# A layer kernel's opening written out anew by pairs of blocks, and a second pool for half of the raw h

## The chip, the cores and the metric

The kernel runs on one core of one Trainium2 chip. The metric is the device time of one execution in microseconds (us); lower is better. The profile is of one execution; the median is of three timed runs.

## The reference, cut to what matters

The layer is a mixer on 1024 tokens of width 2048:

```python
mod = jax.nn.silu(c) @ w_ada[layer] + b_ada[layer]
shift, scale, gate = jnp.split(mod, 3, axis=-1)
h = rms_norm(x, norm_gain[layer]) * (1.0 + scale[:, None, :]) + shift[:, None, :]
proj = h @ w_in[layer]            # (1024 x 2048) @ (2048 x 8192)
...                               # two groups of heads on proj
y = jnp.concatenate([oa, ob], axis=-1).astype(x.dtype) @ w_out[layer]
x = x + (gate[:, None, :] * y).astype(x.dtype)
```

So before the first product with `w_in` there must be the whole `x` (8 MB), its norms, and of `w_ada` (2048 x 6144) the columns of shift and scale for those parts of the width that are used first.

## The kernel before

**The products.** Each big product is made by a Strassen-like scheme with seven products per group of 256 output columns, `P1` to `P7`. Left factors are sums of quarters of h (`A11`, `S3`, `S2`, `A12`, `S1`, `A22`, `S4`; `LEFT` says which product takes which), right factors sums of quarters of the weights (`RIGHT`). Each left factor consists of four tiles of 128x512, one for each pair j = 0 to 3 of 128-blocks of the width (`NP` = 4). Left and right are split in a high and a low part (fp32r), and `mm3` makes three matmuls: high x high, high x low, low x high. One product is 4 pairs x 3 = 12 matmuls, a group 84. `plan` writes the order of products (`flat`) and hangs onto each (product, pair) the making of weights (`Group.make`, `first`, `second`). `run` issues 12 matmuls for a product, does the events, and after each pair calls `tick`, by which loads, stores and side tasks go out in a written order. Groups e (`groups_a`, 16 of them, the first half of the width) come first, then f and g (`groups_b`, second half), h, y and o.

**The opening** (lines 448 to 588). The SP queue loads 32 tiles of x, then `ada_a` tiles: 16 rows for each pair j (each row is 128 x 512 numbers, 256 KB). PE turns x by matmuls against `dg`, diagonal matrices that hold the norms (`turn_x`: 4 matmuls of 128x128 for each of 16 blocks and two halves g of the tokens). For each pair, the 16 rows are weighted with silu(c) and summed: rows 0, 3, 6, 8, 11, 14 by VectorE (`weigh`), rows 5 and 13 by ScalarE and GpSimd, the other 8 by PE (`ada_rows_pe`); `ada_finish` sums over partitions and makes `a_c` and `s_c` (`ada_mod`). `first_half(j)` makes h of the pair (`to_h`, ScalarE), its sums (`combine`, on GpSimd; on VectorE for the last pair), and splits all seven into high and low (`place`: high on ScalarE, L146, low on VectorE, L147). Only after `first_half(3)` does the first group begin: P1, P6, P7, P2, P5. In this stretch only PE's order is as written; the order of the other engines is the scheduler's. From line 599 on every engine's order is as written.

**The seam after groups_a** (lines 657 to 699). While the 16 groups run, side tasks make the second half of h. At the end `gather` places the new left factors as the old ones fall free (`place_later`, at most one in two ticks). Last come `A22` and `S4`: they take the place of factors that are used by the last two products of the last e group, and the raw tiles that they are made of (`a11`, which becomes S2 and then S4, and `a22`) stay in the pool `k1`. The next pool, `hs`, for the heads, takes the same memory; so before it is opened, `until(groups_b[0], "P7")` and `drain()` issue all that is left to place:

```python
    until(groups_b[0], "P7")
    drain()
    k1p2.__exit__(None, None, None)
    k1p.__exit__(None, None, None)
```

Of the kernel before, what the change touches and what calls it, by code (L numbers as in the profile page):

```python
# [17 lines left out]
P = 128  # L18
# [22 lines left out]
ADA_DVE = (0, 3, 6, 8, 11, 14)  # L41
ADA_ACT = (5, 13)
# [17 lines left out]
def layer_kernel(ctx, tc, x, c, w_ada, b_ada, norm_gain, w_in, sb_q_gain, sb_k_gain, ret_norm_gain, w_out,  # L60
# [4 lines left out]
    ctx.enter_context(tc.manual_schedule(engines={mybir.EngineType.PE}))  # L65
# [34 lines left out]
    k1 = k1p.__enter__()  # L100
    stp = tc.tile_pool(name="st", bufs=1)
# [18 lines left out]
    nc.scalar.dma_start(rows[66:74, 0:P], ret_norm_gain.rearrange("o (k p) -> (o k) p", p=P))  # L120
    rows_ps = ps.tile([P, P], F32, tag="C", name="rows_ps")
# [82 lines left out]
    def combine(a11, a12, a21, a22, new, sub):  # L204

        s1, s2, s4 = (new(n) for n in ("S1", "S2", "S4"))
        sub.tensor_tensor(s1, a21, a22, op=ALU.add)
        sub.tensor_tensor(s2, s1, a11, op=ALU.subtract)
        sub.tensor_tensor(a21, a11, a21, op=ALU.subtract)
        sub.tensor_tensor(s4, a12, s2, op=ALU.subtract)  # L210
        return {"A11": a11, "S3": a21, "S2": s2, "A12": a12, "S1": s1, "S4": s4, "A22": a22}

# [54 lines left out]

    sums = []
# [36 lines left out]
    def plan(groups, lasts):  # L305
# [118 lines left out]
    def ada_mod(j, mod):  # L424
# [31 lines left out]

    turns = 0

    def turn_x(kc, g):

        nonlocal turns
        tag, bufs = (("pj0", 1), ("A1", 1), ("pj1", 1), ("pj2", 1), ("B", 1), ("pj3", 1))[turns % 6]
        turns += 1
        tp = ps.tile([P, HALF], F32, tag=tag, bufs=bufs, name=f"xtp_{kc}_{g}")
# [5 lines left out]
        else:  # L470
            xT[kc, g] = k1.tile([P, HALF], F32, tag=f"xT{kc}_{g}", name=f"xT{kc}_{g}")
# [7 lines left out]
    def x_norms(g):  # L479
        for t2 in (4 * g, 4 * g + 2):  # L480
            ss = st.tile([P, 4], F32, tag="ss", bufs=2, name=f"ss_{t2}")
            st6 = st.tile([P, 4, 6], F32, tag="st6", bufs=2, name=f"st6_{t2}")
            mv = st.tile([P, 2], F32, tag="mv", bufs=2, name=f"mv_{t2}")
            for qt in range(4):
                junk = st.tile([P, HALF], F32, tag="ht", bufs=7, name=f"junk_{t2}_{qt}")
                nc.scalar.activation(junk, xt[t2, qt], AF.Square, accum_out=ss[:, qt:qt + 1])
            for qt in range(4):
                nc.vector.bn_stats(st6[:, qt, :], xt[t2 + 1, qt])
            nc.vector.bn_aggr(mv, st6)
            m = st.tile([P, 2], F32, tag="m", bufs=2, name=f"m_{t2}")  # L490
            y = st.tile([P, 2], F32, tag="y", bufs=2, name=f"y_{t2}")
            u = st.tile([P, 2], F32, tag="u", bufs=2, name=f"u_{t2}")
            nc.vector.tensor_reduce(m[:, 0:1], ss, axis=mybir.AxisListType.X, op=ALU.add)
            nc.vector.tensor_scalar(m[:, 0:1], m[:, 0:1], 1.0 / D, EPS, op0=ALU.mult, op1=ALU.add)
            nc.vector.scalar_tensor_tensor(m[:, 1:2], mv[:, 0:1], mv[:, 0:1], mv[:, 1:2], op0=ALU.mult, op1=ALU.add)
            nc.vector.tensor_scalar(m[:, 1:2], m[:, 1:2], EPS, None, op0=ALU.add)
            rsqrt_newton(y, m, u)
            for i in range(2):
                dg[t2 + i] = st.tile([P, P], F32, tag="dg", bufs=8, name=f"dg_{t2 + i}")
                nc.vector.tensor_scalar(dg[t2 + i], ident, y[:, i:i + 1], None, op0=ALU.mult)  # L500

    accs, acc2s, for_pe, row_sums = {}, {}, {}, {}

    def ada_loads(j):

        accs[j] = acc = st.tile([P, HALF], F32, tag="acc", bufs=2, name=f"acc_a{j}")
        tags = free[0][:8] if j == 0 else free[j]
        for r in range(16):
            src = hp.tile([P, HALF], F32, tag=tags[r % len(tags)], name=f"ada_a{j}_{r}")
            nc.sync.dma_start(src.rearrange("p (a n) -> p a n", a=2), ada_rows[:, r, 0:2, 256 * j:256 * j + 256])  # L510
            if r in ADA_DVE:
                weigh(acc, src, r, r == ADA_DVE[0])
# [9 lines left out]
    def ada_rows_pe(j):
        row_sums[j] = sums = ps.tile([P, HALF], F32, tag=("C", "A0")[j % 2], name=f"ada_sums{j}")
        rows_ = for_pe.pop(j)
        for r, src in rows_:
            nc.tensor.matmul(sums[0:1, :], silu_c[:, r:r + 1], src, start=r == rows_[0][0], stop=r == rows_[-1][0])

    def ada_finish(j):
        acc = accs.pop(j)
        nc.vector.tensor_tensor(acc[0:1, :], row_sums.pop(j)[0:1, :], acc[0:1, :], op=ALU.add)  # L530
        mod = ps.tile([P, 4], F32, tag="B", name=f"mod_m{j}")
        over_partitions(mod, [acc, acc2s.pop(j)])
        ada_mod(j, mod)

    def first_half(j):
        for e in range(2):
            for g in range(2):
                to_h(xT[2 * j + e, g], 2 * j + e)
        sums = combine(xT[2 * j, 0], xT[2 * j + 1, 0], xT[2 * j, 1], xT[2 * j + 1, 1],
# [827 lines left out]
```

## Time and profile before

| | us |
|---|---|
| median of three runs | 2012.84 |
| lowest, highest | 2012.56, 2014.52 |
| the profiled execution, its own time | 2010.2 |
| the span in its profile | 2008.4 |
| PE busy | 1932.5 |
| VectorE (DVE) busy | 1460.3 |
| ScalarE (ACT) busy | 866.7 |
| GpSimd (POOL) busy | 189.6 |

The span runs from the first to the last instruction. Matmuls overlap each other, so the record of one (0.39 us) is longer than the distance from one to the next. A matmul of true fp32 (`turn_x`, the `ada` rows) has two records. `PEclk` and the number before "DMA" in a window's row are the granted clock of TensorE: 1.00 is 2.4 GHz, 0.50 is 1.2 GHz.

### The profile page before, as it was taken

The page shows a single profiled execution, that of the slowest core. Times are in us where ns is not written, and L with a number is a line of the kernel's source. Part 1 is how long each engine was busy: PE and PEld are TensorE (multiplying, and loading weights), DVE is VectorE, ACT ScalarE, POOL GpSimd, SP SyncE. Part 2 cuts the span into 40 slices and gives each one's busy share as a digit, 9 for nine tenths or more (in the row PEclk, how much of TensorE's full clock was granted, in tenths as well). Part 3 has the DMA queues.
Part 4 walks back from the last instruction along what each step waited for, and adds up shares of the span by engine and source line. Part 5 has one row for each costly group of instructions (what it writes and reads, how often), then busy time and mean ns, then how long its engine had stood idle before and what let it go on. Part 6 is the DMA issues. An engine that isn't in the chain of part 4 may idle for free. (4 is left out here: it accounts for less than half of the span.)

```text
span 2008.4 us, 26769 instructions
## 1 busy us (share of the span) xinstructions
PE 1932.5 (96%) x9057; PEld 1557.8 (78%) x9057; DVE 1460.3 (73%) x2598; ACT 866.7 (43%) x1574; POOL 189.6 (9%) x131
## 2 busy tenths in 40 slices
PE   5879999999999999999999999899999998999998
PEld 4368888876778787788888888588888887888887
DVE  6778898685668586766656766688787887568765
ACT  4443333553354544454444444434343445345221
POOL 0311111220000001001000100113021211010000
PEclk9879999999999999999999999899999999999999
DMA  9738988434545455443433534758677887357665
GB/s 298 248 119 274 291 283 300 132 110 125 184 152 156 129 169 185 144 133 108 155 114 124 169 104 131 269 189 287 205 265 242 274 273 259 127 168 262 204 206 167
DMA packets 287325, 388.41 MB, mean 193 GB/s; under 512 B 32106, under 2 KB 164276, under 8 KB 287188
## 3 DMA queue, kind: packets, MB, share of 16 engines
q1 hardware_dynamic: 286784, 386.65, 59.5%
q8 instruction: 72, 1.18, 0.3%
q14 instruction: 65, 0.53, 0.1%
q10 hardware_dynamic: 404, 0.05, 0.0%
HBM read 278.51 MB, written 108.10 MB: 192 GB/s over the span
## 5 line engine op out<-in xcount | busy, mean ns | idle before, releaser
L259 ACT ACTIVATE wh_e_P<-wr_e 128x512 fp32r<-128x512 f32 x560 | 353.0, 631 | 464.5 <-PE b_o L151 55.3
L264 DVE TENSOR_TENSOR wl_e_P<-wr_e,wh_e_P 128x512 fp32r<-128x512 f32 x560 | 402.1, 718 | 90.6 <-ACT wh_e_P L259 89.2
L254 DVE TENSOR_TENSOR wr_e<-wr_e,wr_e 128x512 f32<-128x512 f32 x240 | 167.8, 726 | 1.3
L917 DVE TENSOR_TENSOR_SCAN om<-om 128x128 f32<-128x128 f32 (+2 forms) x96 | 95.8, 998 | 55.7 <-ACT om L908 54.1
L443 DVE SCALAR_TENSOR_TENSOR acc_b<-ada_b,silu_c,acc_b 128x512 f32<-128x512 f32 x120 | 90.0, 750 | 17.9 <-DMA ada_b<-in_w_ada_dram 17.1
L730 POOL TENSOR_TENSOR ld<-ld,ld 128x512 f32<-128x512 f32 x7 | 10.3, 1468 | 980.7 <-DMA ld<-mix_A 980.7
L292 DVE TENSOR_TENSOR pt<-b_f,pt 128x512 f32<-128x512 f32 x64 | 44.1, 689 | 57.4 <-PE b_f L152 57.2
L150 PE MATMUL b_e<-S_h,wh_e_P 128*128 128x512 f32 x192 | 76.5, 398 | 5.7 <-ACT pt L286 5.7
L150 PE MATMUL b_h<-S_h,wh_e_P 128*128 128x512 f32 x192 | 78.1, 407 | 1.5 <-ACT S_h L146 1.5
L152 PE MATMUL b_e<-S_h,wl_e_P 128*128 128x512 f32 x192 | 75.9, 396 | 1.2 <-DVE wl_e_P L264 1.2
L964 PE MATMUL oT<-a,v 128*128 128x256 f32 x320 | 76.8, 379 | 0.0
L150 PE MATMUL b_f<-S_h,wh_e_P 128*128 128x512 f32 x192 | 76.6, 399 | 0.0
L151 PE MATMUL b_h<-S_l,wh_e_P 128*128 128x512 f32 x192 | 76.2, 397 | 0.2 <-DVE S_l L147 0.2
L152 PE MATMUL b_h<-S_h,wl_e_P 128*128 128x512 f32 x192 | 75.9, 395 | 0.3 <-DVE wl_e_P L264 0.3
L151 PE MATMUL b_e<-S_l,wh_e_P 128*128 128x512 f32 x192 | 75.8, 395 | 0.0
L150 PE MATMUL b_g<-S_h,wh_e_P 128*128 128x512 f32 x192 | 75.6, 394 | 0.0
L908 ACT ACTIVATE om<-zp,rq 128x128 f32<-128x128 f32 (+2 forms) x96 | 56.0, 583 | 44.9 <-PE zp L903 39.7
L151 PE MATMUL b_f<-S_l,wh_e_P 128*128 128x512 f32 x192 | 75.0, 390 | 0.0
L152 PE MATMUL b_g<-S_h,wl_e_P 128*128 128x512 f32 x192 | 75.0, 390 | 0.0
L152 PE MATMUL b_f<-S_h,wl_e_P 128*128 128x512 f32 x192 | 75.0, 390 | 0.0
L151 PE MATMUL b_g<-S_l,wh_e_P 128*128 128x512 f32 x192 | 74.9, 390 | 0.0
L286 ACT ACTIVATE pt<-b_e 128x512 f32<-128x512 f32 x48 | 28.8, 599 | 97.2 <-PE b_e L152 94.1
(389 smaller groups left out, 5250.0 us busy)
## 6 DMA issues: line engine op xcount, KB each, us to landing
wr_e<-in_w_in_dram SPq DMA_DIRECT2D x128, 512.0 KB
ada_b<-in_w_ada_dram SPq DMA_DIRECT2D x128, 256.0 KB
part<-pt SPq DMA_DIRECT2D x128, 256.0 KB
pt<-part SPq DMA_DIRECT2D x128, 256.0 KB
fin<-pt SPq DMA_DIRECT2D x128, 256.0 KB
ada_a<-in_w_ada_dram SPq DMA_DIRECT2D x64, 256.0 KB
wr_e<-in_w_out_dram SPq DMA_DIRECT2D x32, 512.0 KB
ld<-fin SPq DMA_DIRECT2D x54, 256.0 KB
```

The lines of the kernel that those rows point to most:

```text
L150: nc.tensor.matmul(o, a_hi, b_hi, start=first, stop=False, skip_group_check=True)
L151: nc.tensor.matmul(o, a_hi, b_lo, start=False, stop=False, skip_group_check=True)
L152: nc.tensor.matmul(o, a_lo, b_hi, start=False, stop=last, skip_group_check=True)
L254: eng.tensor_tensor(t[o], t[a], t[b], op=op)
L259: nc.scalar.activation(hi, self.t[RIGHT[p]], AF.Copy)
L264: nc.vector.tensor_tensor(lo, self.t[RIGHT[p]], self.parts[p].bitcast(F32), op=ALU.subtract)
L286: nc.scalar.activation(t, src, AF.Copy, scale=1.0 if gt is None else gt)
L292: nc.vector.tensor_tensor(t, src, t, op=ALU.add)
L443: nc.vector.scalar_tensor_tensor(acc, src, cj, acc, op0=ALU.mult, op1=ALU.add)
L908: nc.scalar.activation(om[:, :n], zp[:, :n], AF.Sigmoid, scale=rq[:, h, 1, i:i + 1])
L917: nc.vector.tensor_tensor_scan(rev, rev, rev, init, op0=ALU.mult, op1=ALU.bypass)
L964: nc.tensor.matmul(ob, v[:, j, :], a[:, cl], start=diag and ib == 0 and b == 0 and j2 == 0, stop=ch == 0 and ib == 2, skip_group_check=True)
```

## The change

Three things change.

1. **The opening.** Every engine's order is as written from the start. Each step is entered in a list `todo` with a time in us (`do(us, fn)`), counted from `landed(n)`, the time at which the n-th load of 256 KB is meant to be there; the list is sorted by these times and issued. The rows of the pairs are loads 32, 48, 68 and 84 on; the weights of the first two groups are loads of their own at `landed(63)` and `landed(99)`. Of the 16 rows of a pair VectorE takes rows 1, 4, 7, 10 (9, 11, 13 in pair 0), PE all others. The sum of a pair goes PE (`ada_close`: the rows' sum plus VectorE's part), ScalarE (a copy of one row), PE (`ada_turn`). GpSimd does nothing here: the sums S1, S3, S2, S4 are VectorE's, in `first_left`.
2. **The first group** begins before the last pair is there: its products P1, P2, P7 for pairs 0 and 1, later for pair 2, and at the end for pair 3 (`first_products`). Its order is P1, P2, P7, P6, P5.
3. **The seam.** Half of the raw second half of h (`a11` and `a22`) lies in a pool `k1x` of its own, which ends after P3 of the first f group. Before `hs` is opened only S1 must have been placed (`while pending("S1")`); A22 and S4 are placed in later ticks. The heads' tiles `R0` to `R5` and `state` move from `hs` to a pool `hsb` in the memory of `k1x`.

```diff
-ADA_DVE = (0, 3, 6, 8, 11, 14)
-ADA_ACT = (5, 13)
+ADA_DVE = (1, 4, 7, 10)
+ADA_DVE_0 = (9, 11, 13)
...
-    ctx.enter_context(tc.manual_schedule(engines={mybir.EngineType.PE}))
+    ctx.enter_context(tc.manual_schedule(engines=set(ENGINES)))
...
+    k1xp = tc.tile_pool(name="k1x", bufs=1)
+    k1x = k1xp.__enter__()
...
-            if i:
-                flat.extend((groups[i - 1], p) for p in ("P4", "P3"))
+            if not i:
+                flat.extend((g, p) for p in ("P2", "P7", "P6", "P5"))
+                continue
+            flat.extend((groups[i - 1], p) for p in ("P4", "P3"))
...
+    def landed(n):
+
+        return 3.5 + 0.8 * (n + 1)
...
-            xT[kc, g] = k1.tile([P, HALF], F32, tag=f"xT{kc}_{g}", name=f"xT{kc}_{g}")
+            xT[kc, g] = (k1x if kc % 2 == g else k1).tile([P, HALF], F32, tag=f"xT{kc}_{g}", name=f"xT{kc}_{g}")
...
+    def ada_load(j, r):
         tags = free[0][:8] if j == 0 else free[j]
+        row_tiles[j, r] = t = hp.tile([P, HALF], F32, tag=tags[r % len(tags)], name=f"ada_a{j}_{r}")
+        nc.sync.dma_start(t.rearrange("p (a n) -> p a n", a=2), ada_rows[:, r, 0:2, 256 * j:256 * j + 256])
+
+    def ada_row(j, r):
+
+        src, on_dve = row_tiles.pop((j, r)), ADA_DVE if j else ADA_DVE_0
+        if r in on_dve:
+            if r == on_dve[0]:
+                accs[j] = st.tile([P, HALF], F32, tag="acc", bufs=1, name=f"acc_a{j}")
+            weigh(accs[j], src, r, r == on_dve[0])
+            return
+        if r == 0:
+            row_sums[j] = ps.tile([P, HALF], F32, tag=("C", "A0")[j % 2], name=f"ada_sums{j}")
+        nc.tensor.matmul(row_sums[j][0:1, :], silu_c[:, r:r + 1], src, start=r == 0, stop=False, skip_group_check=True)
+
+    def ada_close(j):
+
+        nc.tensor.matmul(row_sums[j][0:1, :], ones, accs[j], start=False, stop=True, skip_group_check=True)
+        nc.scalar.activation(accs[j][0:1, :], row_sums.pop(j)[0:1, :], AF.Copy)
+
+    def ada_turn(j):
+
+        mod, acc = ps.tile([P, 4], F32, tag="B", name=f"mod_m{j}"), accs.pop(j)
+        for i in range(4):
+            nc.tensor.matmul(mod[:, i:i + 1], acc[0:1, i * P:(i + 1) * P], ones[0:1, :], start=True, stop=True)
         ada_mod(j, mod)
...
+    def first_left(j, us):
+
+        a11, a21, a12, a22 = (xT[2 * j + e, g] for e in range(2) for g in range(2))
+        last = j == NP - 1
+        s1, s2, s4 = (st.tile([P, HALF], F32, tag="ht", bufs=5, name=f"{n}_{j}") for n in ("S1", "S2", "S4"))
+        tt = nc.vector.tensor_tensor
+        do(us, to_h, a11, 2 * j)
+        do(us, to_h_dve if last else to_h, a12, 2 * j + 1)
+        do(us + 0.1, place, "A11", j, a11)
+        do(us + 0.2, to_h, a21, 2 * j)
+        do(us + 0.2, to_h_dve if last else to_h, a22, 2 * j + 1)
+        do(us + 0.3, place, "A12", j, a12)
+        do(us + 1.0, lambda: tt(s1, a21, a22, op=ALU.add))
+        do(us + 1.0, lambda: tt(a21, a11, a21, op=ALU.subtract))
+        do(us + 1.1, lambda: tt(s2, s1, a11, op=ALU.subtract))
+        do(us + 1.2, place, "S3", j, a21)
+        do(us + 1.3, place, "S2", j, s2)
+        do(us + 2.0, place, "S1", j, s1)
+        do(us + 3.0, lambda: tt(s4, a12, s2, op=ALU.subtract))
+        do(us + 4.0, place, "A22", j, a22)
+        do(us + 5.0, place, "S4", j, s4)
...
+    x_norms(0, landed(15) + 1)
+    x_norms(1, landed(31) + 1)
     for kc in range(KC):
+        do(21.5 + 0.56 * kc, turn_x, kc, 0)
+        do(35.0 + 0.5 * kc if kc < KC // 2 else 42.0 + kc - KC // 2, turn_x, kc, 1)
+
+    at_row = [32, 48, 68, 84]
+    for j in range(NP):
+        for r in range(16):
+            us = landed(at_row[j] + r)
+            do(us - 4, ada_load, j, r)
+            do(us + 0.3, ada_row, j, r)
+        us = landed(at_row[j] + 15) + 0.5
+        do(us, ada_close, j)
+        do(us + 1.5, ada_turn, j)
+        do(us + 2.5, lambda j=j, us=us: first_left(j, us + 2.6))
+    for i in range(2):
+        do(landed(63) - 3.9, groups_a[0].load, i)
+        do(landed(99) - 3.9, groups_a[1].load, i)
+    do(landed(63) + 12, prepare, 1)
+
+    def first_products(js):
+
+        g = groups_a[0]
+        for k, (p, into, i) in enumerate((("P1", "b", 0), ("P2", "a", 3), ("P7", "d", 2))):
...
+            hi, lo = g.parts[p]
+            for j in js:
+                mm3(getattr(g, into), hi[:, j, :], lo[:, j, :], *left[LEFT[p], j], j == 0, j == NP - 1)
...
+    do(landed(63) + 14, first_products, (0, 1))
+    do(landed(83) + 11, first_products, (2,))
...
+    first_products((3,))
+    run_to[0] = 3
...
     until(groups_b[0], "P7")
-    drain()
+    while pending("S1"):
+        tick()
     k1p2.__exit__(None, None, None)
     k1p.__exit__(None, None, None)
...
     groups_o[0].put, groups_o[0].pool = put_y(0), sums
+    until(groups_b[0], "P3")
+    k1xp.__exit__(None, None, None)
+    hsb = hd.enter_context(tc.tile_pool(name="hsb", bufs=1, reuse_waits="tile"))
     until(groups_o[0], "P2")
```

## Rows read from the trace of the kernel before

**Rows 1.** The page: busy time of two engines, and the granted clock.

```profile
PE 1932.5 (96%) x9057; PEld 1557.8 (78%) x9057; DVE 1460.3 (73%) x2598; ACT 866.7 (43%) x1574; POOL 189.6 (9%) x131
...
PEclk9879999999999999999999999899999999999999
```

**Rows 2.** Windows: stretch, its length, each engine's busy time (count), clock, DMA.

```profile
0.00:127.30 127.30, 82.81 (x409) 53.69 (x410) 86.71 (x183) 61.44 (x115) 26.44 (x24) 0.85 0.69 223
127.30:1900.00 1772.70, 1746.88 (x8151) 1419.10 (x8150) 1303.38 (x2308) 785.61 (x1428) 163.20 (x107) 0.99 0.59 192
```

**Rows 3.** Timeline of PE in the opening: start, length, line, operation, count, idle before.

```profile
21.53 22.73 PE L467 MATMUL xtp<-dg,x 128*128 128x128 f32 x188 [5.99 <-DMA x<-in_x_dram]
...
63.02 12.18 PE L526 MATMUL ada_sums<-ada_a,silu_c 128*1 128x512 f32 x28
...
79.17 1.95 PE L421 MATMUL mod_m<-ones,acc_a 128*128 128x1 f32 x16
...
93.87 1.86 PE L526 MATMUL ada_sums<-ada_a,silu_c 128*1 128x512 f32 x2 [5.34 <-DMA ada_a<-in_w_ada_dram]
...
122.29 0.79 PE L150 MATMUL b_e<-S_h,wh_e_P 128*128 128x512 f32 x1 [5.67 <-ACT pt L286]
...
127.34 0.40 PE L150 MATMUL d_e<-S_h,wh_e_P 128*128 128x512 f32 x1
...
132.79 0.39 PE L150 MATMUL b_e<-S_h,wh_e_P 128*128 128x512 f32 x1
```

**Rows 4.** Windows of the opening, columns as in rows 2: the turns, clock and cold products.

```profile
20.00:25.00 5.00, 3.47 (x17) 3.47 (x18) 3.83 (x14) 3.62 (x10) 0.00 (x0) 1.00 1.03 366
25.00:30.00 5.00, 5.00 (x47) 5.00 (x46) 4.49 (x21) 4.01 (x13) 0.00 (x0) 1.00 1.06 380
...
104.80:122.30 17.50, 5.32 (x12) 2.79 (x11) 14.47 (x19) 10.50 (x18) 5.59 (x5) 0.50 0.00 0
122.30:127.30 5.00, 5.00 (x12) 3.97 (x13) 2.09 (x3) 0.45 (x1) 0.73 (x1) 0.53 0.66 210
```

**Rows 5.** Timeline of VectorE in the opening, columns as in rows 3.

```profile
21.19 0.48 DVE L500 TENSOR_SCALAR dg<-ident,y 128x128 f32<-128x128 f32 x2
...
38.04 1.53 DVE L443 SCALAR_TENSOR_TENSOR acc_a<-ada_a,silu_c,acc_a 128x512 f32<-128x512 f32 x2
...
81.42 0.48 DVE L441 TENSOR_SCALAR acc_a<-ada_a,silu_c 128x512 f32<-128x512 f32 x1
...
87.97 3.42 DVE L147 TENSOR_TENSOR S_l<-S,S_h 128x512 fp32r<-128x512 f32 x2
...
104.28 0.55 DVE L428 TENSOR_TENSOR a_c<-a_c,cols 128x2 f32<-128x2 f32 x1
```

**Rows 6.** Timeline of ScalarE: h of a pair, and two high parts.

```profile
63.52 2.93 ACT L435 ACTIVATE xT<-xT,s_c,a_c 128x512 f32<-128x512 f32 x4 [2.37 <-DVE a_c L428]
66.35 1.13 ACT L146 ACTIVATE A_h<-xT 128x512 fp32r<-128x512 f32 x2
```

**Rows 7.** The SP queue: its issues in the opening, and one of its waits.

```profile
0.74 24.21 SPq L455 DMA_DIRECT2D x<-in_x_dram  x32
...
90.99 0.37 SPq L510 DMA_DIRECT2D ada_a<-in_w_ada_dram  x1
...
SPq L510 <- PE ada_sums L526: 9.6, 10, 2.3
```

**Rows 8.** The seam: VectorE's queue, PE behind it, and the clock.

```profile
451.07 2.49 DVE L147 TENSOR_TENSOR A_l<-xT,A_h 128x512 fp32r<-128x512 f32 x4
...
455.89 0.69 DVE L264 TENSOR_TENSOR wl_e_P<-wr_e,wh_e_P 128x512 fp32r<-128x512 f32 x1
...
456.63 0.50 PE L152 MATMUL b_f<-A_h,wl_e_P 128*128 128x512 f32 x1 [1.96 <-DVE wl_e_P L264]
...
461.92 0.39 PE L150 MATMUL d_f<-A_h,wh_e_P 128*128 128x512 f32 x1
...
458.00:460.00 2.00, 2.00 (x3) 0.50 (x2) 1.57 (x3) 1.35 (x3) 0.00 (x0) 0.53 0.84 217
```

More of the change, by code (lines that the diff above doesn't have):

```diff
@@ L100, in layer_kernel @@
     k1 = k1p.__enter__()
+    pp = ctx.enter_context(tc.tile_pool(name="pp", bufs=1))
+    sums = [pp.tile([P, HALF], F32, tag=f"pt{i}", bufs=1, name=f"pt{i}") for i in range(7)]
+    k1xp = tc.tile_pool(name="k1x", bufs=1)
+    k1x = k1xp.__enter__()
     stp = tc.tile_pool(name="st", bufs=1)
@@ L202, in layer_kernel @@
     left = {}
[L204 to L211, printed above, removed]
     def place(n, j, src, eng=nc.vector):
@@ L265, in second @@
             self.parts[p] = self.parts[p], lo
-    sums = []
     def bank(i, name):
@@ L477, in layer_kernel @@
     dg = {}
[L479 to L483, printed above, removed]
-            for qt in range(4):
[L485 to L500, printed above, removed]
@@ L522, in ada_rows_pe @@
[L522 to L532, printed above, removed]
-        ada_mod(j, mod)
@@ new lines, in ada_close, with to_h_dve @@
+    def ada_close(j):
[5 more added lines that the diff above has]
+            nc.tensor.matmul(mod[:, i:i + 1], acc[0:1, i * P:(i + 1) * P], ones[0:1, :], start=True, stop=True)
+        ada_mod(j, mod)
+    def to_h_dve(t, kc):
+        nc.vector.tensor_scalar(t, t, a_c[:, kc:kc + 1], s_c[:, kc:kc + 1], op0=ALU.mult, op1=ALU.add)
@@ L551, in layer_kernel @@
     groups_y = [Group(w_out_k, 0, 256 * i, f"y{i}", put=to_dram(ypart, 2 * i)) for i in range(8)]
+    for g in groups_a + groups_b + groups_c + groups_y:
+        g.pool = sums
     groups_o = [Group(w_out_k, 8, 256 * i, f"o{i}", seed=ypart[2 * i:2 * i + 2]) for i in range(8)]
@@ new lines, in layer_kernel @@
+    at_row = [32, 48, 68, 84]
[8 more added lines that the diff above has]
+        do(us + 2.5, lambda j=j, us=us: first_left(j, us + 2.6))
+    for i in range(2):
+        do(landed(63) - 3.9, groups_a[0].load, i)
+        do(landed(99) - 3.9, groups_a[1].load, i)
@@ L589, in layer_kernel @@
+    do(landed(63) + 14, first_products, (0, 1))
+    do(landed(83) + 11, first_products, (2,))
+    k = 0
+    while k < len(todo):
+        todo[k:] = sorted(todo[k:], key=lambda x: x[:2])
+        todo[k][2]()
+        k += 1
+    first_products((3,))
+    run_to[0] = 3
     stp.__exit__(None, None, None)
-    pp = ctx.enter_context(tc.tile_pool(name="pp", bufs=1))
-    sums.extend(pp.tile([P, HALF], F32, tag=f"pt{i}", bufs=1, name=f"pt{i}") for i in range(7))
-    for g in groups_a + groups_b + groups_c + groups_y:
-        g.pool = sums
@@ L764, in operand @@
     def operand(i, name, dtype=F32R):
-        return hs.pool.tile([P, HALF], dtype, tag=f"R{i}", bufs=1, name=name)
+        return hsb.tile([P, HALF], dtype, tag=f"R{i}", bufs=1, name=name)
     rq = cons.tile([P, NH, 2, NB], F32, name="rq")
@@ L1074, in ret_heads @@
             k, q, v = ks.pop(h), qs.pop(h), vs.pop(h)
-            state = hs.tile([P, NB, P], F32, tag="state", name=f"state_{h}")
+            state = hsb.tile([P, NB, P], F32, tag="state", bufs=1, name=f"state_{h}")
             kds, pTs, ops = {}, {}, {}
```

110 lines of the change are left out of this document (51 added, 59 removed).

## The prediction

> **What bounds the kernel now.** I read the page first: TensorE is busy for 96% of the span with the clock down in slices 2 and 3 and once more in slice 26 [rows 1]. The windows then part the run: from 127.3 us on PE idles 26 us in 1773, in the first 127.3 us 44.5 [rows 2]. So a change of the opening is worth what it does to the moment from which PE runs without a gap; all that follows moves with it. In PE's timeline that moment is 127.34, when P7 of the first group starts with 24 matmuls (P1, P6) behind it [rows 3]. Ahead of it lie two things: the rows of `w_ada`, whose last comes late (PE waits 5.34 us for it, to 93.87), and then 17.5 us (104.8 to 122.3) in which PE is busy for 5.3, at 1.2 GHz, while VectorE is busy for 14.5 [rows 3, 4]. VectorE's timeline shows why: behind `a_c` of pairs 2 and 3 (104.28) it works off the parts of two pairs; and where GpSimd makes the sums, two low parts take 3.42 us instead of 1.2 [rows 5]. The SP queue shows the loads waiting for buffers that PE has yet to free [rows 7].
>
> **Prices.** A turn of x is 8 records of 5.00/47 = 0.106: 0.85 us [rows 4]. A row on PE is two records of 12.18/28 = 0.43: 0.86; the same holds for `ada_close`; `ada_turn` is half of the 16 records in 1.95: about 0.95 [rows 3]. A warm fp32r matmul is (132.79 - 127.34)/24 = 0.227 [rows 3]. VectorE: 2.49/4 = 0.62 for a low part, sum or product of the weights [rows 8], 0.76 for a weighted row, 0.48 for the first one of a pair [rows 5]. ScalarE: 2.93/4 = 0.73 for `to_h`, 0.57 for a high part [rows 6]; the one-row copy isn't in these rows, I take 0.7 with its hand-overs. A load is in use 93.87 - 90.99 = 2.9 us after its issue [rows 3, 7].
>
> **1. The opening: PE's sum.** The change moves 17 rows net to PE (49 instead of 32). PE starts at 21.5 as before [rows 3]; the roots now wait for four tiles and make four `dg` (0.24 each [rows 5]), so 21.9. Its first 3.5 us run at half pace (17 records in 3.47 [rows 4]), 1.8 lost. Then: 32 turns 27.3, 49 rows 42.1, 4 closes 3.4, 4 sum-turns 3.8, 27 first products 6.1; together 82.7, so 21.9 + 1.8 + 82.7 = 106.4. Four times PE must wait for ScalarE's copy (up to 0.7), and `a_c` takes VectorE 0.5: `a_c` of pair 3 stands at 109.7 at the earliest, against 104.8 before [rows 5]. The list's own times (last row landed at 83.5) can't be met by PE.
>
> **The queues in between.** Written order binds VectorE and SP too, so I walk the list.
> Pair 0: 26 turns 22.1, 14 rows 12.0, close, sum-turn: 21.9 + 1.8 + 35.9 = 59.6; VectorE's first row of pair 1 comes ahead of `a_c`, which is there at 60.6.
> Pair 1: 11 rows, 6 turns, close, copy, sum-turn: 59.6 + 17.1 = 76.7; `a_c` 77.2.
> Pair 2: PE does seven rows (to 82.7) and then needs row 11. That tile's buffer is row 1's (ten buffers), and row 1 is VectorE's, behind `first_left(1)`: ScalarE needs 4 `to_h` and 2 high parts (4.1), VectorE then the low part of A12, S1, S3, S2, the low parts of S3 and S2 (3.7), then the row (0.5): 85.5. SP, where all later loads stand behind this one, issues; row 11 is there at 88.4. PE has waited 5.7 us. In the old run the clock was at 1.2 GHz after such a wait (5.34, before 93.87 [rows 3, 4]); I charge 2.2 for it, what 12 matmuls lost at 122.3 to 127.3 (5.0 instead of 2.7 [rows 4]). Rows 11 and 12, then 18 products (4.1), whose weights VectorE ends at 93.1: PE stands at 94.3, rows 13 to 15, close, row 0 of pair 3 (which covers the copy) and sum-turn: 99.8, with the clock 102.0; `a_c` 102.9.
> Pair 3: 8 rows to 108.9; the products of pair 2 need low S3 (102.9 + 4.1 + 3.9 = 110.9), ready 111.3; VectorE has S2, S1, S4, row 7, A22, S4, row 10 to do (4.6): 115.5. Close, copy, sum-turn, `a_c`: 118.6.
> Tail: VectorE waits 1.3 for the first high part, does 11 operations of 0.62 and one short one (0.48) for the last pair, then T1 and the low weights of P6: 9.8 after `a_c`, of which P6's first two matmuls hide 0.5. P6 starts at 118.6 + 9.3 = 127.9 with 36 matmuls done; before, at 122.3 with 12 done [rows 3]. 24 matmuls are 5.4: 127.9 - 122.3 - 5.4 = +0.2. P6 is as cold as before [rows 4], no difference.
> So what GpSimd's removal and the early products save in the tail (17.5 becomes 9.3, and 5.4) is eaten by a sum that comes 13.8 us later. Bounds: no wait in the queues, 109.7 in place of 118.6, gives -8.7; one more wait like pair 2's (5.7 + 2.2) in pair 1 or 3 gives +8.1. I take the walk, because SP's rows show that the loads do wait for PE's rows [rows 7].
>
> The Trainium skill speaks against moving rows to PE: FP8 and Floating Point Precision, TensorE Precision Notes, says that true fp32 takes four passes through the array. By it, an estimate, a row is 4 x 0.227 = 0.91 instead of the measured 0.86, and 49 rows would add 2.4 us. The measured pace decides.
>
> **2. The order P1, P2, P7, P6, P5, and twelve ticks fewer** cost nothing by themselves: the same 84 matmuls, and side tasks start after the opening as before. The bound is one late weight part, 2 us, as at 456.63 [rows 8].
>
> **3. The seam.** `drain()` put the low parts of A22 (four from 451.07) and S4 ahead of the weights of the next f group, which VectorE reached at 455.89; PE waited 1.96 and fell to 1.2 GHz [rows 8]. From 456.63 to 461.92 stand 10 fp32r matmuls and one fp32 with two records (2.3 + 0.9 = 3.2); they took 5.3, so 2.1 went to the clock. After the change those eight parts go out two ticks apart, behind the weights: 4.9 us leave the queue ahead of a wait of 1.96. I take 1.96 + 2.1 = -4.1 off. What is late next is S4, needed by P3 some 10 us later, while VectorE's queue thins out; bounds: -4.1, and 0 if that wait costs the same. The move of the heads' tiles to `hsb` touches only memory that is free by then: 0.
>
> **Sum.** 2010.2 (the profiled execution) + 0.2 - 4.1 = 2006.3. The median lies 2.64 above that execution, so 2009 (2008.9).
>
> **Rivals.**
> *The queue's waits are covered* (the tile of row 11 is there in time; PE alone paces the opening). For: a shorter list of VectorE after `a_c` (the list is 8.3 us long, the seven rows 6.0) would do. Against: the same numbers as they stand. Opening -8.7, seam -4.1: 2000.0.
> *Slower:* the wait on the shared buffer occurs in two pairs instead of one. VectorE's weighted rows stand behind `first_left` in pair 3 as well (row 14 waits for row 4's buffer), and each such wait that outlasts PE's other work costs itself and the cold stretch. It decides when VectorE's list after `a_c` is longer than PE's rows before row 11 or 14 (6 to 7 us). Opening +8.1, seam -4.1: 2016.8, and 2020.9 if S4 takes the seam's gain as well.
> *The seam gives nothing* (S4's late parts make P3 wait in place of P1), opening as walked: 2013.0.
> *Loads pace the opening*, as the list's times have it. 32 loads took 24.21 us to issue [rows 7], 0.76 each; 100 loads to the last row: 0.7 + 76 + 2.9 = 79.6, `a_c` 3.0 later, 82.6, and the end 36 us earlier, 1973. PE's sum of 82.7 from 21.9 speaks against it. DMA: Bandwidth & Descriptors, Anatomy of one DMA, in the Trainium skill says that a DMA's semaphore wait is held on the issuing sequencer; by that the loads can't run ahead of the buffers either, and the SP row agrees.
>
> **How the numbers follow.** A measurement of this kernel tells about 0.2% (4 us) from no change. As walked: 0.45, at 2009, own range 2005 to 2013, a little over half of it within 4 us of the time before. Queues covered 0.2; slower 0.2; seam nothing 0.12; loads 0.03. Faster: 0.45 x 0.45 + 0.2 + 0.03 = 0.43; slower: the slower rival and a bit of the next, less what a smaller size of it leaves: 0.19; the same 0.38. The range takes in the first rival and the slower one: 1999 to 2018.
>
> **What would show it.** In the changed trace: P6 of the first group starting near 128 with 36 matmuls done; PE waiting some 5 us for a row of pair 2, and the row of VectorE that SP waited for; `a_c` of pair 3 near 118 (near 110: first rival; past 123: the slower one); at the seam no wait at P1 of the second f group and the clock at 2.4 GHz. Wrong would be a wait that the opening hands to a later place, or rows on PE that are quicker than 0.86.

## The result and the profile after

The changed kernel takes 2016.9 us (median of 22 runs) against 2008.6 for the kernel before (22 runs as well). The ratio of the runs is 1.0032 [1.0024, 1.0040], so it is slower by 0.3% (6.4 us; the two medians lie 8.3 apart). The forecast was 2009 against the 2012.8 of the three runs of before that were known then, a change of -3.9. The time itself lies inside the range, at its upper end, but the change has the other sign. The profiled execution of after has a span of 2013.1 us against 2008.4, 4.7 more. That is less than the timed runs show, because the profiled execution of before (2010.2) lies 1.6 above its median and that of after (2014.9) lies 2.0 below.

The first fence is from the page of after: the busy time of each engine, and the granted clock in 40 slices.

```profile
PE 1943.4 (97%) x9067; PEld 1550.2 (77%) x9067; DVE 1446.5 (72%) x2579; ACT 862.7 (43%) x1568; POOL 163.9 (8%) x115
...
PEclk9989999999999999999999999999999999999999
```

PE is busier and the clock is better than in [rows 1], so the loss doesn't show in the sums. It shows in the opening. Timeline of PE in the opening of after, columns as in [rows 3]:

```profile
24.25 16.68 PE L474 MATMUL xtp<-dg,x 128*128 128x128 f32 x128 [9.50 <-DVE dg L513]
40.86 5.31 PE L538 MATMUL ada_sums<-ada_a,silu_c 128*1 128x512 f32 x12
...
48.14 1.16 PE L474 MATMUL xtp<-dg,x 128*128 128x128 f32 x8
49.23 1.02 PE L538 MATMUL ada_sums<-ada_a,silu_c 128*1 128x512 f32 x2
50.17 2.05 PE L474 MATMUL xtp<-dg,x 128*128 128x128 f32 x16
...
64.76 1.05 PE L549 MATMUL mod_m<-ones,acc_a 1*128 1x1 f32 x8
...
96.01 2.64 PE L538 MATMUL ada_sums<-ada_a,silu_c 128*1 128x512 f32 x4 [4.41 <-DMA ada_a<-in_w_ada_dram]
...
136.71 0.80 PE L159 MATMUL b_e<-S_h,wh_e_P 128*128 128x512 f32 x1 [3.34 <-ACT wh_e_P L259]
138.73 0.79 PE L161 MATMUL b_e<-S_h,wl_e_P 128*128 128x512 f32 x1 [0.80 <-DVE wl_e_P L264]
144.05 0.79 PE L159 MATMUL b_e<-S_h,wh_e_P 128*128 128x512 f32 x1 [0.69 <-ACT pt L284]
148.81 0.40 PE L159 MATMUL b_e<-A_h,wh_e_P 128*128 128x512 f32 x1
```

PE's unbroken turns begin at 24.25 instead of 21.53 [rows 3]. P6 of the first group starts at 136.71 with 36 matmuls done, instead of at 122.29 with 12. The last row is the first matmul of the second group's first product, which I take as the end of the opening. It stood at 135.51 before, so the opening is 13.3 us longer.

Timelines of VectorE and ScalarE in the opening of after, then two rows of SP's waits (us in total, times, longest). L438 is the first weighted row of a pair on VectorE, L440 a later one:

```profile
14.79 0.23 DVE L132 COPY cols<-rows_ps 128x74 f32<-128x74 f32 x1 [1.18 <-PE rows_ps L131]
...
15.40 2.46 DVE L498 BATCH_NORM_STATS2 st<-x 128x6 f32<-128x512 f32 x4
...
92.77 0.48 DVE L438 TENSOR_SCALAR acc_a<-ada_a,silu_c 128x512 f32<-128x512 f32 x1
...
126.18 0.16 DVE L428 TENSOR_TENSOR a_c<-a_c,cols 128x2 f32<-128x2 f32 x1
...
135.03 0.63 ACT L155 ACTIVATE S_h<-S 128x512 fp32r<-128x512 f32 x1 [1.52 <-DVE A_l L156]
135.56 0.58 ACT L284 ACTIVATE pt<-b_e 128x512 f32<-128x512 f32 x1
136.04 0.62 ACT L259 ACTIVATE wh_e_P<-wr_e 128x512 fp32r<-128x512 f32 x1
```

```profile
SPq L526 <- DVE acc_a L440: 11.4, 3, 6.0
SPq L526 <- DVE acc_a L438: 7.2, 1, 7.2
```

**Where the time went.** Set the same instructions of both timelines of PE side by side, first before, then after: the end of the opening (before alone, for after it stands above), P4 of the last e group, then P1 and P7 of the second f group and P1 of the third:

```profile
135.51 0.39 PE L150 MATMUL b_e<-A_h,wh_e_P 128*128 128x512 f32 x1
...
436.42 0.50 PE L152 MATMUL d_e<-A_h,wl_e_P 128*128 128x512 f32 x1 [1.82 <-DVE wl_e_P L264]
...
454.06 0.39 PE L150 MATMUL b_f<-A_h,wh_e_P 128*128 128x512 f32 x1
...
472.44 0.39 PE L150 MATMUL d_f<-S_h,wh_e_P 128*128 128x512 f32 x1
...
481.78 0.39 PE L150 MATMUL b_f<-A_h,wh_e_P 128*128 128x512 f32 x1
```

```profile
448.67 0.50 PE L161 MATMUL d_e<-A_h,wl_e_P 128*128 128x512 f32 x1 [1.80 <-DVE wl_e_P L264]
...
464.71 0.39 PE L159 MATMUL b_f<-A_h,wh_e_P 128*128 128x512 f32 x1
...
479.95 0.39 PE L159 MATMUL d_f<-S_h,wh_e_P 128*128 128x512 f32 x1
...
489.29 0.39 PE L159 MATMUL b_f<-A_h,wh_e_P 128*128 128x512 f32 x1
```

After minus before: +13.3 at the end of the opening; +12.25 in P4 of the last e group; +10.65 at the first product of the second f group; +7.5 at that of the third. From there it drifts to +6.5 at 1257 us and drops to +4.3 at 1316, and the span differs by 4.7.

The step from 12.25 to 10.65 isn't the seam: behind the same wait of 1.8 us at P4 the granted clock fell in before and didn't in after (windows in the last section). This wait, 1.78 to 1.84 us long, stands in all seventeen profiles of this case. In five of them the clock falls behind it (before, e3, e4, e7, e15) and the way to the second f group takes 17.6 us; in the other twelve it doesn't, and the way takes 16.0. Both happen with the old opening and with the new one, with the old seam and with the new one. So nothing here ties this step to the change.

The step from 10.65 to 7.5 is the seam: the wait of 1.96 and the cold matmuls (at 1.2 GHz) of [rows 8] have no counterpart at this place in after. But 3.1 is less than the seam gives. Where the clock fell at P4, PE reaches the seam later and waits less for VectorE there: 1.96 in before, but 3.19 in e1 and 3.23 in e8, where it didn't fall. Taken between profiles of like clock the seam gives 4.0 to 4.2 (next section).

The late drop lies behind another wait alike in both (2.68 and 2.69, at 1264 and 1271). After it PE runs at 0.427 per matmul for some 6 us in before and some 3 in after, and from 1275 to 1300 the granted clock is 0.89 in before and 1.00 in after. In the other fifteen profiles this wait is 2.5 to 2.8 long, and the slow stretch behind it lasts from nothing (e1, e2, e5, e10) to some 6 us (e6). No run here explains why the clock falls behind one such wait and not behind the next.

So of the 9.0 us between the end of the opening (+13.3) and 1316 us (+4.3), 4.1 are the seam, some 3 are the clock in this pair of profiles (0.6 at P4 and the seam taken together, 2.2 late), and 2 are small drifts that I didn't follow up.

### The profile page after: what moved, and what is told of

It reads as the page before. It is cut to its first block, busy times and chain, and to the rows that moved or that the text cites. A ratio compares the mean times of both kernels' runs of the same rounds, so it can differ in the third digit from the quotient of the medians.

```text
span 2013.1 us, 26743 instructions
## 1 busy us (share of the span) xinstructions
PE 1943.4 (97%) x9067; PEld 1550.2 (77%) x9067; DVE 1446.5 (72%) x2579; ACT 862.7 (43%) x1568; POOL 163.9 (8%) x115
## 5 line engine op out<-in xcount | busy, mean ns | idle before, releaser
L440 DVE SCALAR_TENSOR_TENSOR acc_b<-ada_b,silu_c,acc_b 128x512 f32<-128x512 f32 x120 | 90.0, 750 | 19.2 <-DMA ada_b<-in_w_ada_dram 18.4
```

The source lines that it names most:

```text
L440: nc.vector.scalar_tensor_tensor(acc, src, cj, acc, op0=ALU.mult, op1=ALU.add)
```

## The experiments

**The two halves apart.** e1 has drain() at the seam again, in the changed kernel:

```diff
     until(groups_b[0], "P7")
-    while pending("S1"):
-        tick()
+    drain()
```

> The changed kernel with drain() at the seam as before, so only the opening is changed. Theory: the opening alone costs 12 to 13 us (the offset of the traces at 440 us): 2021, some 4.5 slower than the changed kernel, with the wait of about 2 us and the cold stretch back at P1 of the second f group. Rival (the seam is worth nothing): 2017, as the changed kernel.

Measured: 2021.9, ratio 1.0066 [1.0054, 1.0078]. Timeline of PE and windows (columns as in [rows 2]) of e1:

```profile
464.88 0.39 PE L159 MATMUL b_f<-A_h,wh_e_P 128*128 128x512 f32 x1
...
468.68 0.79 PE L161 MATMUL b_f<-A_h,wl_e_P 128*128 128x512 f32 x1 [3.19 <-DVE wl_e_P L264]
...
484.22 0.39 PE L159 MATMUL d_f<-S_h,wh_e_P 128*128 128x512 f32 x1
```

```profile
465.00:470.00 5.00, 1.81 (x6) 1.19 (x5) 5.00 (x10) 0.74 (x2) 0.00 (x0) 0.85 0.00 0
470.00:475.00 5.00, 5.00 (x16) 2.44 (x16) 2.71 (x5) 2.36 (x4) 0.00 (x0) 0.81 0.88 272
```

The wait and the clock's fall are back. From P1 to P7 of the second f group it takes 19.3 us here and 15.2 in the changed kernel (479.95 - 464.71), and in neither did the clock fall at P4: the seam gives 4.1. The opening alone costs 13.2 in the timed runs (2021.94 - 2008.74).

e7 puts the new seam on the old opening. For the pools to nest, the pool `pp` has to be opened early there too; it holds the tiles `pt`, into which finished sums are copied.

```diff
+    pp = ctx.enter_context(tc.tile_pool(name="pp", bufs=1))
...
+    k1xp = tc.tile_pool(name="k1x", bufs=1)
...
     until(groups_b[0], "P7")
-    drain()
+    while pending("S1"):
+        tick()
...
+    hsb = hd.enter_context(tc.tile_pool(name="hsb", bufs=1, reuse_waits="tile"))
```

> The old opening with the seam of the change: the heads' tiles and half of xT move to pools of their own, and at the change to the second f group only the parts up to S1 are placed at once, those of A22 and S4 two ticks apart. To make room, ht has 5 buffers and the squares' junk goes to PSUM. Theory (the seam gives what was forecast, the opening takes it): no wait at P1 of the second f group, clock at 2.4 GHz behind it, 4.1 to 4.7 us faster than before: 2004 against 2008.6. Rival (the offset of the two traces falls at the seam by chance of the clock, or S4 makes P3 wait): no difference, 2007 to 2010. Fewer ht buffers may cost the opening up to 1 us.

Measured: 1997.7, ratio 0.9946 [0.9934, 0.9958]. That is 11 faster, more than twice what I expected of it, and it beats both kernels. e8 tells the parts apart: pp early, with the old seam. To make room, both e7 and e8 give the tag ht 5 buffers instead of 7 and put the squares' unused output in PSUM.

```diff
+    pp = ctx.enter_context(tc.tile_pool(name="pp", bufs=1))
     stp = tc.tile_pool(name="st", bufs=1)
...
     stp.__exit__(None, None, None)
-    pp = ctx.enter_context(tc.tile_pool(name="pp", bufs=1))
```

> The kernel before with pool pp (the seven pt tiles) opened ahead of the opening's pool st instead of behind it, and, to make room, ht with 5 buffers and the squares' junk in PSUM; the seam as before. Theory (before, the copy of P1's sum to pt waits for the last operation that uses st, since pt lies in its memory, and PE waits 5.67 for that copy ahead of P6): the copy comes at 115, P6 follows P1 without the wait, the opening ends 5 to 6 us earlier: 2003. Rival (the faster opening of the run with the seam came from the seam's pools k1x and hsb or from the seam itself): no difference, 2007 to 2010.

Measured: 2002.6, ratio 0.9963 [0.9950, 0.9975], as expected. The copy of P1's sum on ScalarE, first in the kernel before, then in e8, with PE behind it; last, the wait at the seam of e8:

```profile
121.64 0.60 ACT L286 ACTIVATE pt<-b_e 128x512 f32<-128x512 f32 x1 [0.82 <-DVE S_l L147]
```

```profile
116.54 0.60 ACT L288 ACTIVATE pt<-b_e 128x512 f32<-128x512 f32 x1
...
117.19 0.79 PE L152 MATMUL b_e<-S_h,wh_e_P 128*128 128x512 f32 x1 [0.69 <-ACT pt L288]
...
452.69 0.54 PE L154 MATMUL b_f<-A_h,wl_e_P 128*128 128x512 f32 x1 [3.23 <-DVE wl_e_P L266]
```

P1 of the last pair starts at 114.6 and 114.5, so the smaller room had cost nothing up to there. Then the copy comes 5.1 earlier, and the wait of 5.67 [rows 3] is 0.69. The copy's row in before names VectorE's last low part, which P1's sum doesn't need. So the copy had waited for memory: pt's tiles lay where st's had been, and the pool could only be reused when VectorE had done its last low part. At the end of the opening e8 is 5.1 ahead of the kernel before (130.42 against 135.51).

PE in e7, P1 and P7 of the second f group:

```profile
448.80 0.39 PE L154 MATMUL b_f<-A_h,wh_e_P 128*128 128x512 f32 x1
...
463.20 0.39 PE L154 MATMUL d_f<-S_h,wh_e_P 128*128 128x512 f32 x1
```

From P1 to P7 it takes 14.4 us in e7 and 18.4 in before (472.44 - 454.06), and in both the clock had fallen at P4: the seam gives 4.0. It takes 19.5 in e8 and 15.2 in the changed kernel, and in both the clock had stayed: 4.2. (The difference between e8 and e7, 5.1, mixes the two.) In the timed runs e7 is 4.9 ahead of e8 by the medians. The opening of e7 ends another 0.9 earlier than that of e8, which I didn't follow up.

**The start.** e2 writes the activation of silu_c ahead of the five small loads on ScalarE's queue again.

```diff
+    nc.scalar.activation(silu_c, c_sb, AF.Sigmoid)
     nc.scalar.dma_start(rows[0:16, 0:P], ...)
...
-    nc.scalar.activation(silu_c, c_sb, AF.Sigmoid)
```

> The changed kernel with the activation of silu_c (and its product) written ahead of the five small loads on ScalarE's queue, as it was before the change. Theory (in the changed kernel ScalarE's squares stand behind the issue of those loads until 13.3 us, so the diagonals and with them PE's first turn come at 24.25 instead of 21.53): PE starts at 21.6 to 21.9, all that follows comes 2.4 to 2.7 earlier, since PE has no gap until 91 us: 2014.3. Rival (the later loads or VectorE take the gain back): less than 1 us, 2016 to 2017.

Measured: 2016.5, ratio 1.0036 [1.0022, 1.0050], no change against the changed kernel. PE starts at 24.45: my theory fell. silu_c was ready at 4.4, but VectorE, and with it the statistics of x, still stood behind the copy of the constants to cols. VectorE in e2:

```profile
14.99 0.23 DVE L132 COPY cols<-rows_ps 128x74 f32<-128x74 f32 x1 [10.27 <-PE rows_ps L131]
```

e9 has the edit of e2 and, besides, writes that copy and its followers at 28 us of the list.

```diff
+    do(28.0, small)        # the turn of rows to cols, and kgain, scale_b1
```

> The changed kernel with silu_c ahead of the small loads and, besides, the turn of the small rows into cols and the four operations of VectorE on them written at 28 us of the list instead of at its head. Theory (what holds the start back is not silu_c but VectorE, which stands from 4.7 to 15 us behind the copy to cols, and with it the statistics of x; in the kernel before they began at 8.4): PE's first turn at 21.4 to 21.8 instead of 24.25, and all of that reaches the end, since PE has no gap until 91 us: 2.5 off, 2014.4. Rival (the loads set the pace behind it): PE starts earlier, the end within 1 us of the changed kernel.

Measured: 2014.4, ratio 1.0027 [1.0015, 1.0039], by the medians 2.4 off the changed kernel, with an uncertainty of about 2. PE's timeline in e9:

```profile
21.43 12.92 PE L477 MATMUL xtp<-dg,x 128*128 128x128 f32 x96 [21.43 <-DVE dg L516]
```

The 2.8 us are there at the start, and still at 850 us of the trace. Between 1300 and 1400 us this trace loses them again (0.2 are left at 1393), at waits behind which the profiles differ in the clock anyway. So the start's gain is shown up to there, and the timed gain only just.

**The tail.** e4 writes the last pair's products ahead of that pair's S1, A22 and S4.

```diff
+        if last:
+            do(us + 1.5, first_products, (3,))
         do(us + 2.0, place, "S1", j, s1)
...
-    first_products((3,))
```

> The changed kernel with the last pair's products (and with them the copy of P1's sum and the weights of P6) written ahead of the parts S1, A22 and S4 of that pair instead of behind them; nothing else. Theory (P6's weights come late because the written order puts the copies and the weights behind 6 operations on ScalarE and VectorE that P6 doesn't need; the changed kernel shows PE waiting 3.34 and 0.80 for them): P6 starts at 134 to 134.7 instead of 136.7 and runs without the second wait, 2.5 to 4 us off the end, some more if the clock rises earlier: 2012 to 2014. Rival (P5 waits for S1 instead, or the copy of P1 holds ScalarE): no difference, 2016 to 2017.

Measured: 2011.7, ratio 1.0015 [1.0006, 1.0023], 5.2 off the changed kernel; at the end of the opening the trace is 5.6 ahead. PE in e4, and its clock behind the last of these waits:

```profile
133.59 0.50 PE L159 MATMUL b_e<-S_h,wh_e_P 128*128 128x512 f32 x1
...
134.51 0.69 PE L161 MATMUL b_e<-S_h,wl_e_P 128*128 128x512 f32 x1 [0.19 <-DVE wl_e_P L264]
...
140.39 0.50 PE L159 MATMUL b_e<-S_h,wh_e_P 128*128 128x512 f32 x1 [1.73 <-ACT pt L284]
```

```profile
140.30:143.30 3.00, 2.91 (x13) 2.42 (x14) 2.63 (x3) 0.65 (x3) 1.51 (x1) 1.00 0.64 195
```

P6 starts 3.1 earlier, its first wait (3.34) is gone and its second is 0.19 instead of 0.80. P5 waits 1.73 for a copy but runs at 2.4 GHz, where the changed kernel ran all of P6 and most of P5 at half of it. P6 runs for the most part at half of it in e4 too.

**Both.** e10 joins the edits of e9 and e4.

> The late cols and the last pair's products ahead of its parts S1, A22 and S4, both in one kernel. Theory (start and tail are separate terms of the opening): the gains add, 2.5 + 5.2 = 7.7: 2009.2. Rival (they overlap): 2011 to 2012.

Measured: 2011.0, ratio 1.0009 [0.9999, 1.0019], no longer told apart from the kernel before. In the trace the first addition to a sum comes 6.1 earlier than in the changed kernel, but by 340 us 4.4 are left; of the 7.7 expected, 5.9 came. That is at the edge of the rival's range, so start and tail overlap in part.

**The middle: PE's pace.** e5 writes the turns of the second half of x in a block.

```diff
-        do(35.0 + 0.5 * kc if kc < KC // 2 else 42.0 + kc - KC // 2, turn_x, kc, 1)
+        do(35.0 + 0.25 * kc, turn_x, kc, 1)
```

> The changed kernel with the turns of the second half of x written one behind the other (from 35 us on the list's time, 0.25 apart) instead of alternating with rows of w_ada. The work is the same. Theory (a turn and a row that alternate take 2.03 us in the changed kernel instead of the 0.85 + 0.86 that stretches of one kind take, so some 12 alternations cost 3 to 4 us): a_c of pair 1 stands 2.5 to 4 us earlier, the end too: 2013 to 2014.5. Rival (the pace of PE isn't what counts, since PE waits in pair 2 for VectorE anyway): a_c of pair 1 earlier but the end within 1 us of the changed kernel, 2016 to 2017.5.

Measured: 2020.7, ratio 1.0053 [1.0041, 1.0066]: slower, which neither theory said. PE in e5:

```profile
55.66 5.62 PE L474 MATMUL xtp<-dg,x 128*128 128x128 f32 x48
61.22 1.02 PE L538 MATMUL ada_sums<-ada_a,silu_c 128*1 128x512 f32 x2
...
81.44 1.02 PE L538 MATMUL ada_sums<-ada_a,silu_c 128*1 128x512 f32 x2 [3.15 <-DMA ada_a<-in_w_ada_dram]
```

Six turns in a block take 5.56 up to the next row (61.22 - 55.66). But the edit also puts the turns that stood behind a_c of pair 0 ahead of it, so a_c of pair 0 is 4.7 later. Rows that come later free their buffers later, so the loads of pair 1 come late (3.15), and a_c of pair 1 is 3.8 later instead of earlier. e6 joins this edit to those of e2 and e4:

> The changed kernel with three of the single edits at once: silu_c ahead of the small loads, the turns of the second half in a block, the last pair's products ahead of its parts S1, A22 and S4. Theory (the start, PE's pace and the tail are separate terms of the opening's 12 us): their gains add up, 2.5 + 3 + 5 = 10.5: 2006. Rival (VectorE's list in pairs 1 and 2 sets the end, and what PE gains ahead of it is waited away): 5 to 6 only, 2011.

Measured: 2015.5, ratio 1.0032 [1.0019, 1.0044], -1.4 by the medians and not told apart from the changed kernel. It fits what e4's 5.2 and e5's loss of 3.8 leave.

**The middle: the shared buffer.** e3 gives VectorE the rows 6 to 9, whose buffers no later row of the pair uses.

```diff
-ADA_DVE = (1, 4, 7, 10)
+ADA_DVE = (6, 7, 8, 9)
```

> The changed kernel with VectorE's rows of pairs 1 to 3 being 6 to 9 instead of 1, 4, 7 and 10, so that no load waits for a buffer that VectorE still reads. Theory (PE's wait of 4.41 for row 11 of pair 2 is the reload of row 1's buffer behind VectorE's work on pair 1): that wait goes, a_c of pair 2 stands 4 to 5 earlier, a_c of pair 3 too, and the kernel is 4 to 5 us faster than the changed one: 2012. Rival (the loads are late for another reason, or VectorE's four rows in a block make the close wait instead): less than 2 us, 2015 to 2017.

Measured: 2017.2, ratio 1.0040 [1.0027, 1.0052], no gain. PE in e3, pair 2:

```profile
95.78 0.79 PE L159 MATMUL b_e<-A_h,wh_e_P 128*128 128x512 f32 x1 [3.48 <-ACT wh_e_P L259]
...
99.95 0.80 PE L161 MATMUL b_e<-A_h,wl_e_P 128*128 128x512 f32 x1 [2.95 <-DVE wl_e_P L264]
```

The load's wait of 4.41 is gone, but PE waits 6.4 for the weights of the early products, which VectorE reaches behind the same list. a_c of pair 2 is 3.0 later (112.9) than in the changed kernel. e15 moves the products of pairs 0 and 1 and their weights into pair 3; e13 does that and has e3's rows.

```diff
-    do(landed(63) + 12, prepare, 1)
+    do(landed(83) + 8.5, prepare, 1)
...
-    do(landed(63) + 14, first_products, (0, 1))
-    do(landed(83) + 11, first_products, (2,))
+    do(landed(83) + 11, first_products, (0, 1, 2))
```

> The changed kernel with VectorE's rows being 6 to 9 (no load waits for a buffer that VectorE reads) and, besides, the products of pairs 0 and 1 and the weights of P1, P2 and P7 moved from pair 2 into pair 3, where those of pair 2 stand. Theory (pair 2 is held by VectorE's list behind a_c of pair 1: take the buffer's wait away and PE waits 6.4 for the weights instead, which stand behind the same list; with both away it isn't held): a_c of pair 2 at 97 to 101 instead of 109.9, a_c of pair 3 some 4 to 8 earlier than 126.2, end 4 to 6 faster: 2011 to 2013. Rival (VectorE's rows of pair 2 stand behind the list as well, and the close waits for them): a_c of pair 2 at 103 or later, end less than 3 faster.

> The changed kernel with only the products and weights moved into pair 3; VectorE's rows as in the change, so that the load of row 11 waits for row 1. Theory (the buffer alone holds pair 2 as long as the weights do): PE's wait of 4.4 for row 11 stays, a_c of pair 2 comes 5 earlier (18 products less ahead of it), a_c of pair 3 at most 2 earlier: end within 2 us of the changed kernel. Rival (the early products cost more than the tail wins by them): 3 to 5 faster.

Measured: e13 2024.7, ratio 1.0076 [1.0063, 1.0089]; e15 2025.8, ratio 1.0085 [1.0070, 1.0100]. a_c of pair 2 does come 4.8 earlier in e13 (105.0). It isn't the 97 to 101 of the theory: the close of the sum waits for VectorE's rows, as the rival had it. What was taken from pair 2 is then paid in pair 3, where the weights now stand behind that pair's list. PE in e13, the close of pair 2 and the first product in pair 3:

```profile
99.39 1.15 PE L542 MATMUL ada_sums<-acc_a,ones 128*1 128x512 f32 x2 [3.28 <-DVE acc_a L440]
...
117.40 0.80 PE L159 MATMUL b_e<-A_h,wh_e_P 128*128 128x512 f32 x1 [6.50 <-ACT wh_e_P L259]
```

a_c of pair 3 is 6.9 later (133.0), and 8.0 later in e15. In pair 2, where the change has them, the early products cost less; all four expectations on these two were wrong about the end. In e14 start and tail are mended as well:

> All edits that took a cost away, in one kernel: late cols (start 2.8 earlier), the last pair's products ahead of its other parts (5.2), VectorE's rows 6 to 9 and the products moved into pair 3. Theory (three places, three costs): 2016.9 - 2.5 - 5 - 5 = 2004.4, ahead of the kernel before. Rival (the places overlap): 2008 to 2011, no better than start and tail alone.

Measured: 2015.7, ratio 1.0032 [1.0019, 1.0045]; 4.7 more than e10, which lacks e13's two edits. Both expectations missed it.

**PE's sum against VectorE's lists.** e11 and e12 give VectorE five and three rows of a pair.

```diff
-ADA_DVE = (1, 4, 7, 10)
+ADA_DVE = (1, 4, 7, 10, 13)        # e12: (1, 4, 7)
```

> The changed kernel with five rows of each of the pairs 1 to 3 on VectorE instead of four (row 13 goes back from PE). Theory A (PE's sum sets the opening's end, 0.86 for a row and pair): 3 x 0.86 = 2.6 faster, 2014.3. Theory B (VectorE's lists behind a_c set it): VectorE gets 2.3 more, no gain or up to 2 slower, 2017 to 2019.

> The changed kernel with three rows of each of the pairs 1 to 3 on VectorE instead of four (row 10 goes to PE). Theory A (PE's sum sets the opening's end): 2.6 slower, 2019.5. Theory B (VectorE's lists behind a_c set it): VectorE is 2.3 lighter, no loss or up to 2 faster, 2015 to 2017.

Measured: e11 2017.3, ratio 1.0039 [1.0027, 1.0051]; e12 2016.4, ratio 1.0036 [1.0025, 1.0048]. Three rows more or fewer on PE (2.6 us) move nothing that can be told from none, so theory A is out. In the traces a_c of pair 3 comes 1.5 later with five rows on VectorE and 1.5 earlier with three. That is the sign of theory B, but 0.5 and 0.9 of it are there at a_c of pair 0 already, ahead of the first row that the edits move.

## Why the prediction was wrong

**The seam was right.** Forecast -4.1, from the wait and the cold matmuls of [rows 8]. In after nothing waits at P1 of the second f group, and between profiles of like clock the stretch from P1 to P7 shrinks by 4.0, 4.1 and 4.2. Both the mechanism and the size hold.

**The opening was not: forecast +0.2, measured +13** (13.3 in the trace, 13.2 in the runs of e1). This is the step that failed: the walk of the queues up to P6, and the line that P6 and what follows are as cold as before. At the first product of the second group the opening is 13.1 behind the forecast, term by term:

- *Start, +2.35* (24.25 instead of the 21.9 of the walk). "PE starts at 21.5 as before" allowed for the roots alone, and left out what written order does to VectorE: the copy to cols, which the old opening let the statistics pass, now stands ahead of them (15.40 for the first of them). In e9, without this, PE starts at 21.43. That every engine's order is as written was point 1 of the change, and this is of the kind that the walk was made for.
- *PE's pace, +3.5 up to a_c of pair 0* (66.5 instead of 60.6, less the start). The price of a turn, 0.85, was misread from a window: its 47 records count two that only reach into it, and 45 begin in it [rows 4]. By the starts of the records a turn takes 0.89 in before and after. And a change between turns and rows costs extra: from 48.14 to 50.17 a turn and a row take 2.03 instead of the 1.71 of my prices. The first 16 turns took 16.6 instead of 15.4, the next 10 turns with 14 rows and the close 23.9 instead of 21.4. A row in a block was priced right: six in 5.24, 0.87. The Trainium skill's four passes for true fp32 (FP8 and Floating Point Precision, TensorE Precision Notes) gave an estimate of 0.91 for a row; the trace is near it, and this term isn't the one that failed.
- *Pairs 1 to 3, +1.7* (a_c of pair 3 at 126.2 instead of 118.6, less the above). The walk of the queues held here: the wait for row 11 of pair 2 was there, 4.4 instead of 5.7, and SP did wait for VectorE's row 1 (7.2). (Two figures of the walk are off by a little, 99.8 for 99.6 and 2.2 for the 2.3 of 5.0 - 2.7, which changes nothing.) But the meaning of the wait was misread. I took the buffer for the cause; e3 shows that it is one of two ways in which VectorE's list behind a_c holds PE, and that the rival "queues covered" at -8.7 was not to be had by freeing the buffer.
- *Tail, +1.2, and then +4.3.* P6 came 10.5 behind a_c instead of 9.3. Written order again: on ScalarE the copy of P1's sum (135.56) and P6's high weight (136.04) stand behind the high part of S4 (135.03), and VectorE's work for S1, A22 and S4 stands ahead of that; P6 needs none of the three. "P6 is as cold as before" then missed P6's second wait (0.80) and that P5 waits and is cold too: from P6 to the second group 12.1 us instead of 7.8. e4 takes both terms back by moving one line: 5.6 in the trace, 5.2 in time.

**A misreading behind the whole opening.** I named VectorE's list as what P6 waited for in the kernel before. The row said otherwise: PE waited 5.67 for the copy to pt [rows 3], and that copy waited for the memory of st, which VectorE's last low part held. The change opens pp ahead of st; this is in the full diff, but neither in the three points nor in the lines shown ahead of the prediction, and I gave it no price. Alone it is worth 5 us in the trace and 0.4% in time (e8). Against the old opening with the same pool, the new one thus loses some 18 us in the traces (13.3 + 5.1), not 13, and 19.3 in the timed runs (e1 against e8, both with the old seam).

**The ranking.** The slower rival (the wait in two pairs, 2016.8) came near the time by luck. There was no second wait on a buffer (in pairs 1 and 3 the rows wait 0.3 at most). What made the time were small terms at start, pace and tail, each from written order or from a price misread. Of the 13 us, start and tail are shown by runs (e9 and e4, and e10 gives back 5.9 in time); the pace is read from the traces, and the one run on it, e5, moved other things too. What stays open: why of two waits of 1.8 us one is followed by 1.2 GHz and the other isn't, and what a list of the opening would have to look like in which VectorE doesn't hold PE.

## What to carry to other kernels

When an order made by a scheduler becomes a written one, walk every queue from its first instruction: what an engine used to pass (here a small copy of constants, and a copy of a finished sum) now holds all that stands behind it, and each is a line to move. When a row says that PE waits for a copy, ask what the copy waits for; memory of a pool that is closed late looks like a busy engine. Here opening the next pool early gave 7.6 us by itself, where the whole reordering lost 13. When a pace is taken from a window, count the records that begin in it. Where two engines feed one another through buffers, taking away one wait shows the next one on the same list, so price the list and not the wait.

## What the runs showed of the hardware

A wait of PE of nearly the same length is followed by either clock. Windows behind the 1.8 us at the last e group, in before and in after:

```profile
437.00:441.00 4.00, 4.00 (x12) 3.19 (x11) 4.00 (x7) 1.83 (x5) 0.00 (x0) 0.58 0.47 145
```

```profile
449.00:453.00 4.00, 4.00 (x19) 3.27 (x18) 4.00 (x8) 2.47 (x5) 0.00 (x0) 1.00 0.52 155
```

12 matmuls in 4 us in the one, 19 in the other, on the same work. Over the seventeen profiles the clock in these 4 us is 0.57 to 0.62 in five and 1.00 in the others. P5 of the first group shows it too: behind 1.73 in e4 at 1.00, behind 1.99 in e14 at 0.56. So 2.2 us for a wait, as I charged, is an amount that is there or not. Each kernel was profiled once, so what decides it stays open.

A true fp32 row of 128x512 between turns of 128x128 costs about 0.3 us more than in a block (2.03 for a turn and a row, 0.89 and 0.87 in blocks). Most of it falls where turns give way to a row: from the start of a block of one, two, three or six turns to the row behind it, the traces of after and e5 show 1.09, 1.99, 2.87 and 5.56, which is 0.89 a turn and 0.2 once.
